# The next expert's routing and gather issued ahead of an expert's weight slices, in a mixture-of-experts layer kernel

## Chip, cores, metric

The kernel runs on one core of one Trainium2 chip. The metric is the device time of one execution in microseconds (us); the kernel before takes 2491.59 us (median of 3 runs, 2488.86 to 2494.27).

## What is computed

One layer of a diffusion backbone: a mixer over 2048 latent and 256 context tokens, then an expert-choice mixture of experts (MoE), then a final RMSNorm. The change lies in the MoE alone. Each of 16 experts takes the 256 tokens with its largest affinity, and its rows are added back, scaled by the gate:

```python
cap = EC_CAPACITY * N // N_EXPERTS            # 2 * 2048 // 16 = 256
aff = jax.nn.softmax((h @ w_router + b_router).astype(jnp.float32), axis=-1)
gate, idx = lax.top_k(jnp.swapaxes(aff, 1, 2), cap)
xe = jax.vmap(lambda hb, ib: hb[ib])(h, idx)
hid = jax.nn.silu(jnp.einsum("becd,edf->becf", xe, w_gate)) * jnp.einsum("becd,edf->becf", xe, w_up)
ye = jnp.einsum("becf,efd->becd", hid, w_down) * gate[..., None].astype(h.dtype)
return jax.vmap(lambda ib, yb: jnp.zeros((N, D), yb.dtype).at[ib.reshape(-1)].add(yb.reshape(-1, D)))(idx, ye)
```

## The kernel before

The first 1240 us are the mixer, then a threshold search for the 256 largest affinities of every expert. The MoE follows, expert by expert, all in fp32 precision made of three fp32r products: every operand is split into a rounded high part and the low rest (`mm3`, L193 to L196, three matmuls per product).

What one expert `e` does:

- **Routing**, `route(e)` (L1339): 16 one-hot pieces `oh` on VectorE (L1343), 32 small TensorE matmuls that gather token numbers and gates into the PSUM tile `c` (L1348), then on VectorE `idx` (the 256 token numbers, L1352), `rs` and `gate` (L1354 to L1357). The tiles `idx` and `gate` have two buffers each, `oh` has one.
- **Gather**, the rest of `expert_in(e)`: two indirect DMAs from POOL's queue read 128 rows each of `f_rows` into `xg` (L1373, one buffer).
- **Transposes**: 16 TensorE transposes of `xg` into the PSUM tile `xt` (L1381, two buffers of 4 transposes each), copied out as `xS[0]` by ScalarE (L1383) and `xS[1]` by VectorE (L1384). `xS` has one buffer, so half of the copies wait until the running expert's last gate/up matmul.
- **Gate and up**: `for i in range(2)`: a 512-column slice of each weight, then 4 groups of 48 matmuls into the PSUM tile `gu` (three buffers). ScalarE applies SiLU (`sgl`, L1401), VectorE multiplies (L1402), the result is split into `hS` (L1404, L1405).
- **Down**: two column slices times two halves of the tokens, 24 matmuls each into `dn`, drained by VectorE as `ye` (L1421).
- **Scatter-add**: two indirect DMAs from POOL's queue add `ye` into `h_rows` at the rows that `idx` names (L1458). The second waits until the first has landed.

A weight slice comes in two 1 MB halves: `raw` (two buffers, SP's queue, L177), rounded to `wh` on ScalarE (L183), the rest `wl` on VectorE (L184). `wh` and `wl` have three buffers (pools `wr` and `wx`).

The next expert's input is made inside the running one: `expert` calls `mid()`, which is `expert_in(e + 1)`, between the two passes of the gate/up loop (L1406):

```python
                if mid is not None and i == 0:
                    nx = mid()
```

The order in which each engine's instructions finally stand is set by the tile framework's scheduler, which replays the recorded program in a model of the engines' times. The order on an engine is fixed after that: an instruction that waits holds up all behind it on its engine.

In experts 13 and 14 the final RMSNorm of finished token tiles (`final_tile`, L1482) runs beside the weights; experts 13 to 15 read their rows of `h_rows` (`hr`, L1413) instead of adding in the DMA.

Of the kernel before, what the change touches and what calls it, by code (L numbers as in the profile page):

```python
# [39 lines left out]
def layer_kernel(ctx, tc, x, c, cx, c_ctx, w_mod, b_mod, norm1_g, norm2_g, w_in, conv_w, a_log, dt_bias,  # L40
# [1165 lines left out]

    early.close()
    moe(tc, ctx, locals())


def moe(tc, ctx, env):
# [6 lines left out]
    with ExitStack() as pd:  # L1218
# [120 lines left out]
        def route(e):  # L1339
            oh = ohp.tile([P, 2, 8, 256], BF, name="oh", bufs=1)  # L1340
            for s in range(2):
                for g in range(8):
                    nc.vector.tensor_scalar(oh[:, s, g, :], siob, SL[:, s, e, g:g + 1], None, op0=OP.is_equal)  # L1343
            rp = ps_c.tile([P, 2, 256], F32, name="c")
            for hf in range(2):
                for i in range(16):
                    s, g = divmod(i, 8)
                    nc.tensor.matmul(rp[:, hf, 0:5], oh[:, s, g, hf * P:(hf + 1) * P], vals[:, s, e, g, :],  # L1348
                                     start=(i == 0), stop=(i == 15))
            idx = rt.tile([P, 2], I32, name="idx", bufs=2)  # L1350
            with nc.allow_low_precision(reason="token numbers are whole"):
                nc.vector.tensor_reduce(idx, rp[:, :, 0:2], axis=AX.X, op=OP.add)  # L1352
            rs = rt.tile([P, 2, 5], F32, name="rs", bufs=2)
            nc.vector.tensor_copy(rs, rp[:, :, 0:5])  # L1354
            gate = rt.tile([P, 2], F32, name="gate", bufs=2)
            nc.vector.tensor_tensor(gate, rs[:, :, 2], rs[:, :, 3], op=OP.add)
            nc.vector.tensor_tensor(gate, gate, rs[:, :, 4], op=OP.add)  # L1357
            return idx, gate
# [3 lines left out]
        def next_w(src):  # L1362
            if pre:
                return pre.pop(0)
            pool = wx if nchunk[0] % 3 == 2 else wr
            nchunk[0] += 1
            return load_w(raw_p, pool, src)

        def expert_in(e):
            idx, gate = route(e)  # L1370
            xg = wk.tile([P, 2, D], F32, name="xg", bufs=1)
            for hf in range(2):
                last[1] = nc.gpsimd.indirect_dma_start(out=xg[:, hf, :], out_offset=None, in_=f_rows,  # L1373
                                                       in_offset=bass.IndirectOffsetOnAxis(ap=idx[:, hf:hf + 1], axis=0))
            xS = [wk.tile([P, KT, 256], F32R, name=f"xS{s}", bufs=1) for s in range(2)]
            for kk in range(4):
                ps = ps_t.tile([P, 2, 256], F32, name="xt")
                for k2 in range(2):
                    for hf in range(2):
                        k = 2 * kk + k2  # L1380
                        nc.tensor.transpose(ps[:, k2, hf * P:(hf + 1) * P], xg[:, hf, k * P:(k + 1) * P], ident)  # L1381
                ks = slice(2 * kk, 2 * kk + 2)
                nc.scalar.activation(xS[0][:, ks, :], ps, AF.Copy)  # L1383
                last[0] = nc.vector.tensor_tensor(xS[1][:, ks, :], ps, xS[0][:, ks, :].bitcast(F32), op=OP.subtract)  # L1384
            return idx, gate, xS

        def expert(e, st, mid=None):
            idx, gate, xS = st
            nx = None
            hS = [wk.tile([P, KT, 256], F32R, name=f"hS{s}", bufs=1) for s in range(2)]  # L1390
            for i in range(2):
                gw = next_w(w_gate[0, e, :, i * 512:(i + 1) * 512])
                uw = next_w(w_up[0, e, :, i * 512:(i + 1) * 512])
                for f in range(4):
                    fs = slice(f * P, (f + 1) * P)
                    pg = ps_a.tile([P, 2, 256], F32, name="gu")
                    for j, w in enumerate((gw, uw)):
                        for k in range(KT):
                            mm3(pg[:, j, :], w[0][:, k, fs], w[1][:, k, fs], xS[0][:, k, :], xS[1][:, k, :], k, KT)
                    sg_ = wk.tile([P, 256], F32, name="sgl", bufs=2)  # L1400
                    nc.scalar.activation(sg_, pg[:, 0, :], AF.Silu)  # L1401
                    nc.vector.tensor_tensor(sg_, sg_, pg[:, 1, :], op=OP.mult)  # L1402
                    ff = 4 * i + f
                    nc.scalar.activation(hS[0][:, ff, :], sg_, AF.Copy)  # L1404
                    nc.vector.tensor_tensor(hS[1][:, ff, :], sg_, hS[0][:, ff, :].bitcast(F32), op=OP.subtract)  # L1405
                if mid is not None and i == 0:  # L1406
                    nx = mid()
            ye = wk.tile([P, 2, D], F32, name="ye", bufs=1)
            if e >= NE - NLAST:
                hr = wk.tile([P, 2, D], F32, name="hr", bufs=1)  # L1410
# [71 lines left out]
        def final_tile(t):  # L1482
            ht = wk.tile([P, D], F32, name="ht", bufs=2)
            nc.sync.dma_start(ht, h_rows[t * P:(t + 1) * P, :])
            final_norm(ht, ht)
            nc.sync.dma_start(out[t * P:(t + 1) * P, :], ht)

        last = [None, None]
        st = expert_in(0)
        with tc.issue_after(last[1].ins):  # L1490
            pre.append(load_w(raw_p, wx, w_gate[0, 0, :, 512:1024], cast=C2))
        for e in range(NE):
            nx = mid = None
            if e + 1 < NE:
                if e in MIDE:
                    mid = lambda: expert_in(e + 1)
                else:
                    nx = expert_in(e + 1)
            for t in FTS.get(e, ()):
                final_tile(t)  # L1500
            st = expert(e, st, mid) or nx
# [98 lines left out]
```

## Time and profile before

| | us |
|---|---|
| median of 3 runs | 2491.59 (2488.86 to 2494.27) |
| the profiled execution | 2491.46 |
| its span | 2489.7 |
| TensorE busy in it | 2360.5 (95%), 16841 matmuls |
| VectorE, ScalarE, POOL busy | 1580.0, 1120.1, 516.9 |
| granted TensorE clock, mean | 0.973 |

The span is the time from the first to the last instruction in the trace. The profiled execution's own time is 1.76 us more than its span. Busy times are shares of the whole; what a stage is bound by is read from that stage. In the rows further down, a bracket at a row's end gives the idle time of that engine just before the row and what ended it.

### The profile page before, as it was taken

Reading aid. Unit: us, or ns where it says so; the run is one execution under the profiler, and the core shown is the slowest. Engines: PE = TensorE matmul, PEld = TensorE weight load, DVE = VectorE, ACT = ScalarE, POOL = GpSimd, SP = SyncE. Lnnn points to the kernel's source line nnn. Section 1 sums busy time; section 2 is a strip of 40 time slices with the busy share of each in tenths; the row PEclk is TensorE's granted clock in tenths of the full one; section 3 lists DMA queues with packets and bytes.
Section 4 is the critical chain, followed back from the end, with each engine's and each line's share of the span. In section 5 each row is a group of like instructions: output and inputs, shape, how many; then the busy total and the mean of one; then the engine's idle time right before and its main releaser. Section 6 shows DMA issues by size and latency. Waiting matters only on the chain.

```text
span 2489.7 us, 43138 instructions
## 1 busy us (share of the span) xinstructions
PE 2360.5 (95%) x16841; PEld 2160.1 (87%) x16841; DVE 1580.0 (63%) x3335; ACT 1120.1 (45%) x2008; POOL 516.9 (21%) x451
## 2 busy tenths in 40 slices
PE   7999999998988989999949999999999999999998
PEld 5999999887777888888838899999999999998897
DVE  7688755557879546566774556555565565556675
ACT  4554555567633444333332444444444444444453
POOL 2321222211112553232250101101111011111211
PEclk9999999999999999999978999999999999999999
DMA  8676655399856998655463666666676666668894
GB/s 262 200 232 199 216 164 171 124 269 323 266 127 192 253 276 235 199 180 182 166 201 111 203 187 215 199 208 207 203 220 196 210 217 199 209 205 266 300 300 166
DMA packets 487994, 526.59 MB, mean 212 GB/s; under 512 B 103887, under 2 KB 409880, under 8 KB 485742
## 3 DMA queue, kind: packets, MB, share of 16 engines
q1 hardware_dynamic: 470238, 463.27, 59.0%
q0 software_dynamic: 17120, 59.77, 8.3%
q8 instruction: 133, 2.18, 0.4%
q10 hardware_dynamic: 432, 0.79, 0.1%
q14 instruction: 71, 0.58, 0.1%
HBM read 400.45 MB, written 123.31 MB: 210 GB/s over the span
## 4 chain that ended last, share of the span: by engine, by line
PE 56%; DMA 14%; DVE 7%; ACT 4%; issue 3%; SPq 1%; POOL 1%; POOLq 0%; DVEq 0%; ACTq 0%
PE gu L196 6%; PE gu L195 6%; PE gu L194 6%; DMA xg<-f_rows,idx 4%; PE dn L195 4%; PE dn L194 4%; PE dn L196 4%; PE mx L194 2%; PE mx L195 2%; PE mx L196 2%; ACT wh L183 2%; PE pj L194 1%; PE pj L195 1%; PE pj L196 1%; DVE wl L184 1%
## 5 line engine op out<-in xcount | busy, mean ns | idle before, releaser
L184 DVE TENSOR_TENSOR wl<-raw,wh 128x2048 fp32r<-128x2048 f32 (+1 forms) x214 | 450.3, 2116 | 297.5 <-ACT wh L183 297.3
L194 PE MATMUL gu<-xS,wh 128*128 128x256 f32 x2048 | 582.3, 285 | 5.9 <-ACT wh L183 4.7
L196 PE MATMUL gu<-xS,wl 128*128 128x256 f32 x2048 | 580.8, 286 | 4.7 <-DVE wl L184 4.7
L195 PE MATMUL gu<-xS,wh 128*128 128x256 f32 x2048 | 582.1, 285 | 0.0
L183 ACT ACTIVATE wh<-raw 128x2048 fp32r<-128x2048 f32 (+1 forms) x218 | 381.6, 1771 | 361.3 <-DMA raw<-in_w_gate_dram 145.6
L194 PEld LDWEIGHTS gu<-xS,wh 128*128 128x128 f32 x2048 | 395.7, 193 | 8.0 <-ACT wh L183 5.3
L196 PEld LDWEIGHTS gu<-xS,wl 128*128 128x128 f32 x2048 | 394.5, 193 | 6.4 <-DVE wl L184 5.4
L195 PEld LDWEIGHTS gu<-xS,wh 128*128 128x128 f32 x2048 | 396.0, 193 | 1.1
L194 PE MATMUL pj<-aS,wh 128*128 128x258 f32 x832 | 239.2, 291 | 3.5 <-DVE y L460 3.1
L195 PE MATMUL pj<-aS,wh 128*128 128x258 f32 x832 | 239.9, 290 | 0.2 <-DVE aS L358 0.2
L196 PE MATMUL pj<-aS,wl 128*128 128x258 f32 x832 | 239.3, 289 | 0.9 <-DVE wl L184 0.9
L1458 POOL DMA_INDIRECT h_rows<-ye,idx x26 | 66.8, 2568 | 660.7 <-DVE ye L1421 567.8
L194 PE MATMUL dn<-wh,hS 128*128 128x512 f32 (+1 forms) x520 | 202.7, 390 | 0.0
L195 PE MATMUL dn<-wl,hS 128*128 128x512 f32 (+1 forms) x520 | 201.2, 387 | 0.4 <-DVE wl L184 0.4
L196 PE MATMUL dn<-wh,hS 128*128 128x512 f32 (+1 forms) x520 | 200.3, 386 | 0.0
L194 PEld LDWEIGHTS pj<-aS,wh 128*128 128x128 f32 x832 | 158.2, 192 | 5.0 <-issue 2.8
L195 PEld LDWEIGHTS pj<-aS,wh 128*128 128x128 f32 x832 | 160.1, 193 | 0.6 <-DVE aS L358 0.4
L196 PEld LDWEIGHTS pj<-aS,wl 128*128 128x128 f32 x832 | 159.3, 192 | 1.3 <-DVE wl L184 1.1
L194 PE MATMUL uv<-wh,ast 128*128 128x512 f32 x384 | 154.1, 401 | 0.0
L196 PE MATMUL uv<-wh,ast 128*128 128x512 f32 x384 | 151.2, 394 | 0.0
L195 PE MATMUL uv<-wl,ast 128*128 128x512 f32 x384 | 150.9, 393 | 0.0
L1404 ACT ACTIVATE hS<-sgl 128x256 fp32r<-128x256 f32 x128 | 53.1, 414 | 176.6 <-DVE sgl L1402 176.4
(480 smaller groups left out, 4547.3 us busy)
## 6 DMA issues: line engine op xcount, KB each, us to landing
raw<-in_w_gate_dram SPq DMA_DIRECT2D x64, 1024.0 KB
raw<-in_w_up_dram SPq DMA_DIRECT2D x64, 1024.0 KB
raw<-in_w_down_dram SPq DMA_DIRECT2D x64, 1024.0 KB
kv<-kv SPq DMA_DIRECT2D x140, 256.0 KB
raw<-in_w_mod_dram SPq DMA_DIRECT2D x18, 1024.0 KB
a_sp<-aS SPq DMA_DIRECT2D x32, 512.0 KB
ast<-a_sp POOLq DMA_DIRECT2D x16, 1024.0 KB, 7.8
raw<-in_w_in_dram SPq DMA_DIRECT2D x12, 1024.0 KB
```

What stands on the lines that cost most here:

```text
L183: nc.scalar.activation(wh[:, ks, s:s + 256], raw[:, ks], AF.Copy)
L184: (lo_eng or nc.vector).tensor_tensor(wl[:, ks, s:s + 256], raw[:, ks], wh[:, ks, s:s + 256].bitcast(F32), op=OP.subtract)
L194: pace(nc.tensor.matmul(ps, ah, bh, start=(k == 0), stop=False), after)
L195: nc.tensor.matmul(ps, ah, bl, start=False, stop=False)
L196: return nc.tensor.matmul(ps, al, bh, start=False, stop=(k == nk - 1))
L1404: nc.scalar.activation(hS[0][:, ff, :], sg_, AF.Copy)
L1458: nc.gpsimd.indirect_dma_start(out=h_rows, out_offset=bass.IndirectOffsetOnAxis(ap=idx[:, hf:hf + 1], axis=0), in_=ye[:, hf, :], in_offset ...
```

## The change

`expert_in(e)` is cut in two. The first part (routing and the gather) keeps the name and returns `idx`, `gate`, `xg`. The second, `turn`, holds the transposes and their copies. `expert` calls the first part ahead of its first weight slice, and `turn` where `mid()` was called.

```diff
@@ expert_in
             for hf in range(2):
                 last[1] = nc.gpsimd.indirect_dma_start(out=xg[:, hf, :], out_offset=None, in_=f_rows,
                                                        in_offset=bass.IndirectOffsetOnAxis(ap=idx[:, hf:hf + 1], axis=0))
+            return idx, gate, xg
+
+        def turn(idx, gate, xg):
             xS = [wk.tile([P, KT, 256], F32R, name=f"xS{s}", bufs=1) for s in range(2)]
...
@@ expert
             hS = [wk.tile([P, KT, 256], F32R, name=f"hS{s}", bufs=1) for s in range(2)]
+            g = mid() if mid is not None else None
             for i in range(2):
...
                 if mid is not None and i == 0:
-                    nx = mid()
+                    nx = turn(*g)
@@ the loop over experts
-        st = expert_in(0)
+        st = turn(*expert_in(0))
...
-                    nx = expert_in(e + 1)
+                    nx = turn(*expert_in(e + 1))
```

Lines behind the new `return` stand 3 or 4 higher in the changed kernel (`ye` is L1425 there, `sgl` L1406, `hS` L1409, the transposes L1384).

Experts 0 and 1 keep their order, since the scheduler had already put the routing of experts 0, 1 and 2 ahead of expert 0's weights. In experts 2 to 12 the same piece repeats, so it is shown once.

VectorE, from the fourth `ye` of expert 3 into the first gate/up groups of expert 4, before (the semaphores DMASW count transfers of POOL's queue, DMAHW those of SP's queue; `idx` is that of expert 5):

```order
L1421 SCALAR_TENSOR_TENSOR ye<-dn,gate,gt2r 128x512 [waits PE_49]
L184 TENSOR_TENSOR wl<-raw,wh 128x8x256 [waits DMAHW4_49,Activation_49]
L184 TENSOR_TENSOR wl<-raw,wh 128x8x256 [waits DMAHW5_49,Activation_49]
L1402 TENSOR_TENSOR sgl<-sgl,gu 128x256 [waits Activation_49]
L1405 TENSOR_TENSOR hS_16801<-sgl,hS_16800 128x256 [waits Activation_49]
L1402 TENSOR_TENSOR sgl<-sgl,gu 128x256 [waits Activation_49]
L1405 TENSOR_TENSOR hS_16801<-sgl,hS_16800 128x256 [waits Activation_49]
L1402 TENSOR_TENSOR sgl<-sgl,gu 128x256 [waits Activation_49]
L1405 TENSOR_TENSOR hS_16801<-sgl,hS_16800 128x256 [waits Activation_49]
L184 TENSOR_TENSOR wl<-raw,wh 128x8x256 [waits DMAHW6_49,PE_49,Activation_49]
L1352 TENSOR_REDUCE idx<-c 128x2 [waits DMASW2_49,DMASW1_49,DMASW3_49,DMASW0_49,PE_49]
L1354 COPY rs<-c 128x10
```

The same place in the changed kernel:

```order
L1425 SCALAR_TENSOR_TENSOR ye<-dn,gate,gt2r 128x512 [waits PE_49]
L1343 TENSOR_SCALAR oh<-siob,SL 128x256 [waits PE_49]
L1343 TENSOR_SCALAR oh<-siob,SL 128x256 x15
L184 TENSOR_TENSOR wl<-raw,wh 128x8x256 [waits DMAHW4_49,Activation_49]
L1352 TENSOR_REDUCE idx<-c 128x2 [waits DMASW2_49,DMASW3_49,DMASW1_49,DMASW0_49]
L1354 COPY rs<-c 128x10
L184 TENSOR_TENSOR wl<-raw,wh 128x8x256 [waits DMAHW5_49,Activation_49]
L1356 TENSOR_TENSOR gate<-rs 128x2 [waits DVE_49]
L1406 TENSOR_TENSOR sgl<-sgl,gu 128x256 [waits Activation_49]
L1357 TENSOR_TENSOR gate<-gate,rs 128x2 [waits DVE_49]
L1409 TENSOR_TENSOR hS_16801<-sgl,hS_16800 128x256 [waits Activation_49]
```

`idx` moved from behind three drained gate/up groups and three weight halves to behind one weight half, with a `wl` and all drains of the gate/up groups now behind it. It waits for the same four transfers of POOL's queue in both.

TensorE, where the last run of routing matmuls of an expert begins (`gu` is gate/up, `dn` down), before, in the middle of the first gate/up pass:

```order
L194 MATMUL gu<-xS_17098,wh 128x256
L195 MATMUL gu<-xS_17099,wh 128x256
L196 MATMUL gu<-xS_17098,wl 128x256
L1348 LDWEIGHTS oh
L1348 MATMUL c<-vals,oh 128x5
```

and in the changed kernel, behind the last down matmul of the expert before:

```order
L194 MATMUL dn<-wh,hS_16109 128x512
L195 MATMUL dn<-wl,hS_16109 128x512
L196 MATMUL dn<-wh,hS_16110 128x512
L1348 LDWEIGHTS oh
L1348 MATMUL c<-vals,oh 128x5
```

Before, 9 of an expert's 32 routing matmuls stand between two down groups and 23 behind some 190 gate/up matmuls; now 18 and 8 stand between down groups and 6 behind the last.

TensorE at the first transposes of an expert's input, before:

```order
L194 MATMUL gu<-xS_16407,wh 128x256
L195 MATMUL gu<-xS_16408,wh 128x256
L1381 MATMUL xt<-ident,xg 128x128 x2
L196 MATMUL gu<-xS_16407,wl 128x256
L194 MATMUL gu<-xS_16407,wh 128x256
```

and in the changed kernel:

```order
L195 MATMUL gu<-xS_16408,wh 128x256
L196 MATMUL gu<-xS_16407,wl 128x256
L1384 MATMUL xt<-ident,xg 128x128 x8
L194 MATMUL gu<-xS_16407,wh 128x256
L195 MATMUL gu<-xS_16408,wh 128x256
```

Before, two transposes stand behind 272 of the running expert's 384 gate/up matmuls and six more 11 matmuls later; now all eight of the first half stand behind exactly 192 of them. On POOL the order of scatter-adds and gathers is the same in both: two scatter-adds of one expert, then two gathers. On SP only some halves and token tiles of experts 13 to 15 change places.

## Rows read from the trace of the kernel before

**Rows 1.** Busy time by stretch: expert 1, experts 2 to 12, start of the tail.
```profile
core 0: us, PE busy (x) PEld busy (x) DVE busy (x) ACT busy (x) POOL busy (x), PEclk, DMA share, GB/s
1382.79:1457.98 75.19, 71.83 (x498) 67.37 (x497) 38.57 (x41) 30.31 (x32) 6.74 (x4) 0.98 0.63 196
1457.98:2240.75 782.77, 779.14 (x5809) 733.58 (x5807) 462.08 (x616) 334.07 (x352) 98.16 (x44) 1.00 0.67 207
2240.75:2312.00 71.25, 67.91 (x509) 64.19 (x508) 43.80 (x61) 32.36 (x43) 12.33 (x11) 0.98 0.83 272
```
**Rows 2.** TensorE's waits, 1457.98 to 2240.75 us: total, times, longest.
```profile
PE xt L1381 <- DMA xg<-f_rows,idx: 3.4, 7, 1.0
```
**Rows 3.** Timeline of VectorE: first a run of one-hots, then expert 1.
```profile
1324.24 3.21 DVE L1343 TENSOR_SCALAR oh<-siob,SL 128x256 bf16<-128x256 bf16 x16
...
1398.75 0.75 DVE L1421 SCALAR_TENSOR_TENSOR ye<-dn,gate,gt2r 128x512 f32<-128x512 f32 x1 [1.26 <-PE dn L196]
1401.18 2.29 DVE L184 TENSOR_TENSOR wl<-raw,wh 128x2048 fp32r<-128x2048 f32 x1 [1.68 <-ACT wh L183]
1411.82 0.16 DVE L1352 TENSOR_REDUCE idx<-c 128x2 int32<-128x4 f32 x1 [8.35 <-DMA h_rows<-ye,idx]
...
1414.45 0.41 DVE L1402 TENSOR_TENSOR sgl<-sgl,gu 128x256 f32<-128x256 f32 x1
```
**Rows 4.** Timeline of POOL, expert 1.
```profile
1394.90 1.62 POOL L1458 DMA_INDIRECT h_rows<-ye,idx  x1 [63.30 <-DVE ye L1421]
1403.42 1.58 POOL L1458 DMA_INDIRECT h_rows<-ye,idx  x1 [6.90 <-DMA h_rows<-ye,idx]
1412.77 2.58 POOL L1373 DMA_INDIRECT xg<-f_rows,idx  x1 [7.77 <-issue]
```
**Rows 5.** Timeline of TensorE, expert 1: its waits and the stretch behind them.
```profile
1414.92 0.39 PE L194 MATMUL gu<-xS,wh 128*128 128x256 f32 x1 [1.23 <-DVE sgl L1402]
...
1422.21 0.30 PE L1381 MATMUL xt<-ident,xg 128*128 128x128 f32 x1 [1.27 <-DMA xg<-f_rows,idx]
1423.38 0.98 PE L1381 MATMUL xt<-ident,xg 128*128 128x128 f32 x7 [0.86 <-DMA xg<-f_rows,idx]
1424.11 0.36 PE L194 MATMUL gu<-xS,wh 128*128 128x256 f32 x1
...
1427.69 0.32 PE L196 MATMUL gu<-xS,wl 128*128 128x256 f32 x1
```
**Rows 6.** Busy time by stretch, expert 1: right behind the waits, and later.
```profile
1424.20:1427.50 3.30, 3.30 (x19) 3.30 (x18) 0.98 (x3) 0.45 (x2) 0.00 (x0) 0.52 1.07 359
1428.00:1448.00 20.00, 20.00 (x170) 20.00 (x168) 7.17 (x9) 7.55 (x10) 0.00 (x0) 1.00 0.41 134
```
**Rows 7.** Timeline of POOL: a scatter-add pair of the long form, one of the short.
```profile
1613.38 3.42 POOL L1458 DMA_INDIRECT h_rows<-ye,idx  x1 [41.54 <-DVE ye L1421]
1624.69 2.33 POOL L1458 DMA_INDIRECT h_rows<-ye,idx  x1 [7.88 <-DMA h_rows<-ye,idx]
1639.60 1.07 POOL L1373 DMA_INDIRECT xg<-f_rows,idx  x1 [12.59 <-DVE rs L1354]
...
1684.30 1.62 POOL L1458 DMA_INDIRECT h_rows<-ye,idx  x1 [40.88 <-DVE ye L1421]
1691.84 2.52 POOL L1458 DMA_INDIRECT h_rows<-ye,idx  x1 [5.92 <-DMA h_rows<-ye,idx]
```
**Rows 8.** Timeline of VectorE: the fourth `ye` beside each of these pairs.
```profile
1616.55 0.75 DVE L1421 SCALAR_TENSOR_TENSOR ye<-dn,gate,gt2r 128x512 f32<-128x512 f32 x1 [1.23 <-PE dn L196]
...
1687.67 0.75 DVE L1421 SCALAR_TENSOR_TENSOR ye<-dn,gate,gt2r 128x512 f32<-128x512 f32 x1 [0.19 <-PE dn L196]
```
**Rows 9.** DMA issues, the scatter-add at 1624.69 us: median us to landing.
```profile
h_rows<-ye,idx POOLq DMA_INDIRECT x1, 9.8
```
**Rows 10.** TensorE's waits from 2240.75 us to the end.
```profile
PE gu L194 <- ACT wh L183: 4.7, 3, 3.2
PE gu L196 <- DVE wl L184: 4.7, 4, 1.5
```

## The prediction

> **What bounds the kernel now.** I first read busy time by stretch, cut at the same TensorE instruction of each expert. In the eleven experts 2 to 12 TensorE is busy 779.14 of 782.77 us, 70.8 of 71.2 us per expert, at a granted clock of 1.00 [rows 1]. VectorE is busy 42 us of such an expert. TensorE's waits there are all of one kind, transposes that wait for the gathered rows, 3.4 us in seven waits [rows 2]. So the wait that the change aims at is worth 3.4 us in this stretch, and what else it costs TensorE counts in full.
>
> Expert 1 takes 75.19 us, though it has no routing matmuls [rows 1]; its routing was already done ahead, and its `idx` already stands early on VectorE, behind a single weight half. Its timelines are therefore the changed order in small. `idx` could not be written at 1403.5, when VectorE came to it: it waited 8.35 us for the second scatter-add of expert 0 to land [rows 3]. The reason is the buffer: `idx` has two, so the numbers for expert e+1 go where those of expert e-1 are, which the scatter-adds of e-1 still read. Behind `idx` stood the drains of the gate/up groups. TensorE filled its three `gu` buffers, waited 1.23 us, reached the transposes, and waited 1.27 and 0.86 us more, since the gather could only leave at 1412.77, behind `idx` [rows 4, 5]: 3.36 us idle. Behind that the granted clock was 0.52, the lower of its two levels, and 17 intervals of gate/up matmuls took 3.58 us, 0.21 each, where 0.118 is normal (170 in 20 us) [rows 5, 6]: 1.6 us more.
>
> **The change part by part.** The matmuls, transposes, drains and transfers are the same in number. Four things move.
>
> 1. The gather. Before, it left at 1639.60 in an expert whose fourth `ye` began at 1616.55, 23.0 us behind [rows 7, 8]. I call that start D; it follows the last down matmul at once. The gather cannot leave before `idx`, and `idx` not before the scatter-adds have landed (time R). Expert 1: R is 1411.82, D is 1398.75, R is D+13.1 [rows 3].
>
> 2. The transposes move further than the gather does. In the new order 6 routing matmuls (some 0.2 us) and 144 gate/up matmuls stand ahead of the first one that needs a drained buffer: at 0.118 us that is D+17.2. The transposes stand behind 192: D+22.8. Before, 272 stood ahead of them.
>
> 3. `idx` in front of the drains. In expert 1 TensorE goes on 3.1 us behind R (1414.92) and has all gathered rows 11.56 us behind R (1423.38) [rows 3, 5]. So idle time per expert is R+11.56, less D+22.8, less 0.5 of useful transposing and pipeline between: R minus D minus 11.7.
>
> How large is R-D in experts 2 to 12? Their scatter-adds leave at the same point of the expert before and after the change, so the old rows tell. There are two forms. Long, in 8 of these 11: the first leaves at D-3.2, POOL needs 3.42 us for it, the second leaves 11.3 later at D+8.1 [rows 7, 8]. It lands after 9.8 us there [rows 9], after 8.4 us in expert 1, where VectorE stood still beside it [rows 3, 4]. In the new order VectorE stands still then, so I take 8.4: R is D+16.5, idle 4.8 us (6.2 with 9.8). Short, in 3 of 11: the first at D-3.4, the second 7.5 later at D+4.2 [rows 7, 8]; VectorE is then writing one-hots and a weight half, so I take 9.8: R is D+14.0, idle 2.3 us (0.9 with 8.4). The clock: a long one idles more than expert 1 did, so it pays 1.6 us; for a short one, between that and the waits of up to 1.0 us that cost no clock [rows 1, 2], half, 0.8. The ends are 0 and 3.2.
>
> Sum: 8 x (4.8 + 1.6) + 3 x (2.3 + 0.8) = 60.5 us, less the 3.4 us of old waits: +57. Expert 1's own idle and clock in all eleven would be 11 x 5.0 - 3.4 = +51, so the two agree.
>
> 4. What else moves. Sixteen one-hots (3.2 us [rows 3]) now stand ahead of a weight half right behind D. That half is needed only for the second gate/up pass, past D+22, so they cost nothing; were they late, it would be 3.2 us per expert. The weight stream stands while VectorE waits, from about D+6.5 to R, since `raw` is freed by `wl`. In expert 1 it stood 8.35 us and caught up: TensorE's waits in that expert are the three above. I take nothing, and price it below. In expert 13 the same `idx` waits once more; there weights already made TensorE wait (4.7 + 4.7 us from 2240.75 to the end [rows 10]), and a few weight halves and token tiles change places on SP. I take +2, between -4 (all gather waits of the tail gone and some weights earlier) and +8 (as for a long one in expert 13, and a little more). Experts 0 and 1 do not change.
>
> 2491.46 for the profiled execution, +57, +2: **2550 us**. The median of the runs is 0.13 us above the profiled execution, which changes nothing.
>
> **The rivals.** *The short form everywhere.* Whether the first scatter-add is long shows in VectorE's order: where a `wl` had begun before POOL's instruction, POOL took 3.42 us, else 1.62. With VectorE shifted, all eleven might be short: 11 x (2.3 + 0.8) - 3.4 + 2 = +33, 2524; with the quickest landing and no clock loss 11 x 0.9 - 3.4 = +6.5, 2498. Against it: the weight halves beside D hang on the second gate/up pass, in which nothing is held up. The Trainium skill (SBUF — State Buffer, Who interferes with whom) infers that VectorE's `tensor_tensor` does not hold up POOL's descriptor writing; by that rule the short form would hold everywhere. The two durations speak against it here.
>
> *The wait is hidden: not slower.* If the scatter-adds landed before VectorE comes to `idx` at about D+6.5 (fourth `ye` 0.75, one-hots 3.2, `wl` 2.3), nothing would stand still, the gather would leave 16 us earlier than now, and all old gather waits would go: 2491.5 - 4 = 2487. It decides at two landings of under 5 us each; the rows show 8.5 and 8.4 [rows 3, 4] and 11.3 and 9.8 [rows 7, 9]. The Trainium skill (DMA: Bandwidth & Descriptors, Anatomy of one DMA) fits 2.0 us plus bytes over 436 GB/s for a DMA of POOL's queue; my estimate from it is 3.2 us for 128 rows of 4 KB, and so this rival's time. The measured landings are over twice that, so it gets little.
>
> *The weight stream does not catch up.* `wl` behind `idx` comes 10 us later, the next `raw` with it, and TensorE waits for weights in each expert, as it does in the tail. The tail's 9.4 us lie in about three experts, 3 us each: 11 x 3 on top, 2583. For it: 10 us of stopped stream against 71.2 us for twelve halves; against it: expert 1.
>
> *The change does little.* The scheduler could have left the order as it was; the order rows show that `idx` and the transposes moved in eleven experts and that both wait for the same things as before, so this has no weight of its own.
>
> **How the numbers follow.** Forecast (long forms mostly) 0.66, 2515 to 2580; all short 0.18, 2498 to 2524; hidden 0.05, about 2487; weights late 0.11, 2570 to 2600. The range leaves out the hidden case, the lowest third of the short one and the upper half of the weights' case: 2505 to 2588. A measurement of this kernel can tell 0.2%, 5 us. Slower by more than that: all but the hidden case and a little of the short one, 0.93; within it 0.05; faster 0.02, since even all gather waits are only 4 us.
>
> **What would show it.** In the changed profile VectorE's waits list `idx` behind the scatter-add some 13 times, 7 to 10 us each, about 115 us in all, and TensorE's list the drain `sgl` and the gathered rows, about 48 us together; experts 2 to 12 take 74 to 77 us each, with a granted clock of 0.97 to 0.99. The gathers leave about 1 us behind each `idx`. I am wrong if those experts stay under 72 us, if `idx` waits but TensorE does not, or if TensorE's new waits are for `wh` and `wl`.

## The result, and the profile after

| | before | changed |
|---|---|---|
| median of 4 runs each, us | 2490.23 (2484.49 to 2494.27) | 2516.78 (2512.46 to 2521.0) |
| profiled execution, us | 2491.46 | 2519.66 |
| its span | 2489.7 | 2517.8 |
| experts 2 to 12 | 782.77 | 813.10 |
| from there to the end | 248.95 | 245.8 |

The change makes the kernel slower: ratio 1.0098, 95% interval 1.0079 to 1.0117. (Ratios are given here as they are on record with the runs; they differ from the quotient of the two medians, 1.0107 here, by up to 0.15%.) By the spans it costs 28.1 us: 30.3 in experts 2 to 12, 0.9 ahead of them, and 3.1 given back in the tail. The forecast had 59 us, over twice that.

Busy time by stretch (columns as in [rows 1]): experts 2 to 12, the start of the tail, then experts 4 and 8 alone and 3.3 us behind the transposes of each.

```profile
1458.90:2272.00 813.10, 789.12 (x5810) 733.96 (x5809) 461.19 (x617) 334.80 (x352) 89.78 (x44) 1.00 0.65 200
2272.00:2343.25 71.25, 67.87 (x514) 63.66 (x513) 45.11 (x64) 32.79 (x40) 12.21 (x11) 1.00 0.82 270
1605.18:1679.21 74.03, 71.53 (x530) 66.46 (x528) 42.22 (x57) 30.43 (x32) 8.37 (x4) 1.00 0.65 199
1900.24:1977.12 76.88, 72.98 (x529) 67.94 (x528) 42.08 (x57) 30.43 (x32) 8.49 (x4) 0.98 0.63 192
1647.20:1650.50 3.30, 3.30 (x30) 3.30 (x29) 2.08 (x3) 0.42 (x1) 0.00 (x0) 1.00 0.93 304
1943.60:1946.90 3.30, 3.30 (x19) 3.30 (x18) 0.84 (x3) 0.54 (x2) 0.00 (x0) 0.55 1.08 366
```

Against [rows 1] TensorE idles 23.98 us in the eleven experts (813.10 less 789.12) where it idled 3.63, and is busy 789.12 us where it was busy 779.14. So the 30.3 us are 20.35 of additional idle time and 9.98 of the same matmuls taking longer. The last two rows show a part of the second: behind the waits of expert 8 the granted clock was 0.55, the lower level, with 19 matmuls in 3.3 us; behind those of expert 4 it was 1.00, with 30.

What TensorE waited for in experts 2 to 12 (total, times, longest):

```profile
PE xt L1384 <- DMA xg<-f_rows,idx: 14.1, 15, 2.2
PE gu L194 <- DVE sgl L1406: 9.3, 11, 1.7
```

The first row answers to [rows 2], 3.4 us in seven waits; the second is new. What VectorE waited for at `idx`, from 1300 us to the end:

```profile
DVE idx L1352 <- DMA h_rows<-ye,idx: 73.0, 8, 10.2
DVE idx L1352 <- issue: 41.6, 5, 9.2
```

That is 114.6 us in 13 waits. "issue" means that the profile shows no releaser for five of them; they stand in the same place and are of much the same length. In the first of them `idx` starts at 1709.29 us, and the second scatter-add, which POOL begins at 1699.10, lands 10.1 us later, so there too `idx` follows the landing at once.

Expert 4 shows the chain. VectorE's timeline, from the fourth `ye` of expert 3 on:

```profile
1619.94 0.75 DVE L1425 SCALAR_TENSOR_TENSOR ye<-dn,gate,gt2r 128x512 f32<-128x512 f32 x1 [0.21 <-PE dn L196]
1620.61 3.22 DVE L1343 TENSOR_SCALAR oh<-siob,SL 128x256 bf16<-128x256 bf16 x16
1624.07 2.29 DVE L184 TENSOR_TENSOR wl<-raw,wh 128x2048 fp32r<-128x2048 f32 x1 [0.24 <-ACT wh L183]
1636.12 0.16 DVE L1352 TENSOR_REDUCE idx<-c 128x2 int32<-128x4 f32 x1 [9.77 <-DMA h_rows<-ye,idx]
```

POOL's timeline of the same expert:

```profile
1617.79 3.44 POOL L1462 DMA_INDIRECT h_rows<-ye,idx  x1 [51.23 <-DVE ye L1425]
1628.94 1.59 POOL L1462 DMA_INDIRECT h_rows<-ye,idx  x1 [7.71 <-DMA h_rows<-ye,idx]
1637.07 2.37 POOL L1373 DMA_INDIRECT xg<-f_rows,idx  x1 [6.54 <-issue]
1639.74 0.97 POOL L1373 DMA_INDIRECT xg<-f_rows,idx  x1 [0.30 <-issue]
```

TensorE's waits in it:

```profile
1639.02 0.39 PE L194 MATMUL gu<-xS,wh 128*128 128x256 f32 x1 [1.59 <-DVE sgl L1406]
1645.08 0.30 PE L1384 MATMUL xt<-ident,xg 128*128 128x128 f32 x1
1646.25 0.98 PE L1384 MATMUL xt<-ident,xg 128*128 128x128 f32 x7 [0.86 <-DMA xg<-f_rows,idx]
```

D (the start of the fourth `ye`) is 1619.94. The second scatter-add leaves 9.0 us later, and `idx` follows its landing at 1636.12, which is R, D+16.2. VectorE stands still for 9.77 us until then, the drains behind `idx` start 2.4 us later, and TensorE, out of `gu` buffers, goes on 2.9 behind R. The gather leaves 0.95 behind R and its last rows are there 10.13 behind R (1646.25).

### The profile page after: what moved, and what is told of

The parts are those of the page before. It is cut to its first block, busy times and chain, and to the rows that moved or that the text cites. A ratio compares the mean times of both kernels' runs of the same rounds, so it can differ in the third digit from the quotient of the medians.

```text
span 2517.8 us, 43148 instructions
## 1 busy us (share of the span) xinstructions
PE 2371.0 (94%) x16841; PEld 2159.3 (86%) x16841; DVE 1581.7 (63%) x3335; ACT 1121.7 (45%) x2008; POOL 510.9 (20%) x451
## 5 line engine op out<-in xcount | busy, mean ns | idle before, releaser
L194 PE MATMUL gu<-xS,wh 128*128 128x256 f32 x2048 | 583.8, 286 | 14.8 <-DVE sgl L1406 11.0
```

The source lines that it names most:

```text
L194: pace(nc.tensor.matmul(ps, ah, bh, start=(k == 0), stop=False), after)
```

## Experiments

The theory: `idx` has two buffers, so it waits until the scatter-adds that still read the old numbers have landed; VectorE, TensorE and the gather stand behind it, and everything else about the change is harmless. The first rival: the transposes have come too far forward, whatever `idx` does. The second: a cost of the new order itself, on TensorE or in the weight stream. The kernel before was run again beside each group: 2495.26 us (e1 to e4), 2497.05 (e5 to e8), 2495.22 (e9, e10). The ratios compare with these runs.

**e1: a third buffer for `idx` in the changed kernel.**

```diff
-            idx = rt.tile([P, 2], I32, name="idx", bufs=2)
+            idx = rt.tile([P, 2], I32, name="idx", bufs=3)
```

> The changed kernel with three buffers of idx instead of two, so that the numbers of expert e+1 no longer overwrite those that the scatter-adds of expert e-1 still read. Theory (the wait of idx for the scatter-adds, through its two buffers, is what costs): VectorE's waits no longer list idx behind the scatter-add, TensorE's waits for the drain sgl go, experts 2 to 12 fall from 73.9 us to 71 us, and the time to 2482 to 2492. The gathers still stand behind the second scatter-add on POOL, so a remainder of gather waits of up to 1 us per expert is allowed. Rival (the early gather itself, beside scatter-adds and weight loads, or the one-hots ahead of the weight half, slow the expert): it stays at 2510 to 2520.

Measured: 2471.84 us (2467.76 to 2477.09), ratio 0.9914, interval 0.9894 to 0.9934: 45 us under the changed kernel, and faster than the kernel before. The two waits of expert 4 above are gone in experts 2 to 12; TensorE is never idle in experts 2 to 12 (busy time by stretch, those experts):

```profile
1450.66:2222.00 771.34, 771.34 (x5800) 717.10 (x5799) 461.69 (x617) 335.45 (x352) 85.68 (x44) 1.00 0.67 210
```

VectorE around one `idx`:

```profile
1535.39 0.75 DVE L1425 SCALAR_TENSOR_TENSOR ye<-dn,gate,gt2r 128x512 f32<-128x512 f32 x1 [0.51 <-PE dn L196]
1536.06 0.15 DVE L1352 TENSOR_REDUCE idx<-c 128x2 int32<-128x4 f32 x1
```

and POOL:

```profile
1532.50 1.58 POOL L1462 DMA_INDIRECT h_rows<-ye,idx  x1 [58.88 <-DVE ye L1425]
1536.48 1.07 POOL L1373 DMA_INDIRECT xg<-f_rows,idx  x1 [2.40 <-DVE rs L1354]
1537.86 1.02 POOL L1373 DMA_INDIRECT xg<-f_rows,idx  x1 [0.30 <-issue]
1540.45 3.08 POOL L1462 DMA_INDIRECT h_rows<-ye,idx  x1 [1.57 <-DMA h_rows<-ye,idx]
```

`idx` is written 0.67 us behind D, and the gather leaves between the two scatter-adds instead of behind both. The scheduler did more with the buffer than drop a wait: it moved the routing one step further ahead. So the worth of the buffer has two parts, the wait that is gone and that new order. The result is 10 us better than the low end of what I expected, which needs the next runs.

**e2: the third buffer in the kernel before**, with nothing else changed.

> The kernel before with three buffers of idx. Theory: only expert 1 had the wait there, so expert 1 falls from 75.2 us (75.8 with routing matmuls) to about 71 us and the time by 4 to 5 us, to about 2486; the old gather waits of experts 2 to 12 (3.4 us) stay. Rival (expert 1 was slow for another reason, as the start of the stage): no change, 2490.

Measured: 2484.02 us (2481.29 to 2492.89), ratio 0.9970, 0.9957 to 0.9983. As expected, there is little to gain: in the old order the wait of `idx` for a scatter-add stands in expert 1 alone, and there it is gone. The gain is 7 us by the ratio, above the 4 to 5 expected; e6 below shows that the third buffer's shift of the tiles gives about as much by itself.

**e3: the scatter writes instead of adding**, in the changed kernel, so the scatter lands sooner and `idx` still waits for it. The sum over the experts is left out, so the kernel no longer computes the layer; the order of instructions on every engine is that of the changed kernel.

```diff
-                                                 in_=ye[:, hf, :], in_offset=None, compute_op=OP.add)
+                                                 in_=ye[:, hf, :], in_offset=None)
```

> The changed kernel with scatters that write instead of add (the sum over experts is left out), in the same order of instructions on every engine. Theory (the landing of the two scatter-adds sets when idx can be written): if a plain scatter lands sooner, at 4 to 6 us each instead of 11 and 6.5, idx waits 0 to 3 us instead of 9, TensorE waits for nothing new, and the time is 2485 to 2497. If it lands as late as with the add, the time stays near 2515 and idx waits as long. Rival (the wait of idx is not what TensorE loses its time to): idx waits less and the time stays.

Measured: 2483.95 us (2475.75 to 2489.13), ratio 0.9953, 0.9938 to 0.9968. VectorE's and TensorE's waits from 1300 us to the end:

```profile
DVE idx L1352 <- DMA h_rows<-ye,idx: 63.4, 12, 6.7
DVE idx L1352 <- issue: 3.0, 1, 3.0
PE xt L1384 <- DMA xg<-f_rows,idx: 4.9, 5, 1.9
```

VectorE still waits 66 us at `idx`, in the longer ones over twice the 0 to 3 us each that I expected, and yet TensorE waits only 4.9 us for gathered rows, 0.6 of it in experts 2 to 12. So VectorE's wait is not what costs; what costs is the part of it that outlasts TensorE's stock of work. In expert 4 of this kernel R is D+12.8, 3.4 us sooner than with the add, and TensorE is not idle there at all. The order on VectorE and TensorE is that of the changed kernel, and the kernel is no slower than the one before, which speaks against the second rival. What the plain scatter saves by itself is not told apart here.

**e4: the transposes behind 218 gate/up matmuls instead of 192**, one group into the second pass as the scheduler lays it out.

```diff
-                if mid is not None and i == 0:
-                    nx = turn(*g)
+                    if mid is not None and i == 1 and f == 0:
+                        nx = turn(*g)
```

> The changed kernel with the transposes one group later: behind 218 gate/up matmuls of an expert instead of 192, 3.1 us later on TensorE. Theory: the gathered rows land about 26 us behind the last down matmul, TensorE then comes at about 27 us, so the waits for the gather (14 us in experts 2 to 12) and the two drops of the clock go, the waits for the drain (9 us) and that of idx stay: 2497 to 2505. Rival (TensorE loses its time to the drains alone, and the gather's waits only take over what would be lost anyway): 2512 to 2518.

Measured: 2497.55 us (2490.1 to 2504.91), ratio 1.0006, 0.9991 to 1.0021. Waits from 1300 us to the end:

```profile
DVE idx L1352 <- DMA h_rows<-ye,idx: 70.4, 8, 9.8
DVE idx L1352 <- issue: 42.8, 5, 9.3
PE gu L194 <- DVE sgl L1406: 7.7, 10, 1.6
PE xt L1384 <- DMA xg<-f_rows,idx: 2.9, 2, 1.9
```

`idx` waits as long as in the changed kernel (113.2 us), the transposes no longer wait in experts 2 to 12, and 19 us come back by the medians, 23 by the ratios. So the first rival has a part: 26 matmuls, 3 us of work, decide whether a late gather is seen.

**e5 to e10: is it the buffer, or where it pushes the tiles?** By the program's layout the third `idx` buffer takes 32 bytes per partition, and `oh`, `xg`, `xS`, `hS`, `sgl` and `ye` stand 32 bytes further on. In e1 the matmuls themselves had changed: gate/up ran quicker, down slower. So e5 and e6 add 32 unused bytes to the changed kernel and to the one before, with the same instructions in the same order on every engine:

```diff
-        SL = rt.tile([P, 2, NE, 8], F32, name="SL", bufs=1)
+        SL = rt.tile([P, 2 * NE * 8 + 8], F32, name="SL", bufs=1)[:, 0:256].rearrange("p (s e g) -> p s e g", s=2, e=NE)
```

e5, the changed kernel with it:

> The changed kernel with two idx buffers and the same instructions in the same order on every engine; only SL is 32 bytes longer per partition, so that xS, hS, xg and ye start 32 bytes further on, where the third idx buffer put them. In the trace of e1_idx3 a gate/up matmul takes 116.5 ns and a down matmul 235.1, against 120.4 and 229.7 in the changed kernel. Theory A (the place of the tiles sets these times, not the third buffer and not the order): gate/up 116 to 117 ns, down 233 to 236; the first pass is hidden behind the wait for the scatter-add in any case, so per expert only the second pass gains, 192 x 3.9 ns = 0.75 us, against 96 x 5.4 = 0.5 us lost: 2510 to 2518, idx waits as before, TensorE's waits longer by some 8 us. Theory B (order or buffer): 120 ns and 2515 to 2520.

Measured: 2513.98 us (2509.2 to 2518.73), ratio 1.0077, 1.0056 to 1.0099. Costliest groups of TensorE from 1440 to 2240 us (matmuls, busy us, mean ns of one), the changed kernel:

```profile
L195 PE MATMUL gu<-xS,wh 128*128 128x256 f32 x1373 | 389.4, 284 | 0.0
L195 PE MATMUL dn<-wl,hS 128*128 128x512 f32 x352 | 137.3, 390 | 0.0
```

and e5:

```profile
L195 PE MATMUL gu<-xS,wh 128*128 128x256 f32 x1395 | 389.9, 280 | 0.0
L195 PE MATMUL dn<-wl,hS 128*128 128x512 f32 x352 | 139.2, 395 | 0.0
```

Matmuls overlap, so a mean includes the pipeline; from start to start e5's take about 117 ns (gate/up) and 235 (down) against 120 and 230. Neither the order nor the buffer does this, since both are those of the changed kernel. The `idx` wait stays (111.8 us), and with it the loss; TensorE's waits for gathered rows and for the drain together grow by 0.8 us, where I had put down some 8.

e6, the kernel before with it:

> The kernel before with the same 32 bytes and nothing else. Theory A: gate/up 117.5 ns instead of 120.5, down 233 instead of 227.6, so per expert 384 x 3.0 ns less and 96 x 5.5 ns more, 0.6 us less; times 16 experts about 10 us: 2480 to 2486, as with the third idx buffer, which then had no worth of its own there but expert 1's wait. Theory B (the third buffer or the order): the time of before, 2490 to 2495, with 120.5 ns.

Measured: 2492.0 us (2481.24 to 2495.78), ratio 0.9974, 0.9958 to 0.9990. The matmuls changed as expected (about 117 and 234 ns), the time by half of what I had put down: it is above the 2480 to 2486 expected. TensorE's waits for gathered rows, from 1300 us to the end:

```profile
PE xt L1381 <- DMA xg<-f_rows,idx: 17.4, 17, 2.1
```

In the kernel before, the same view has 8.9 us in 12 waits: a TensorE that is sooner at the transposes waits longer there for a gather that leaves no sooner, which would account for the half that is missing.

e7, three `idx` buffers and the 32 bytes (64 further on in all), and e9, the same with 96 bytes (128 further on):

> The changed kernel with three idx buffers and the 32 bytes more, so that xS and hS stand at a multiple of 64 bytes again, as in the kernel before and the changed one; the order is that of e1_idx3. This takes the worth of the buffer apart from that of the place. Theory A: gate/up 119 to 120.5 ns, down 228 to 230, 0.8 us more per expert than e1_idx3: 2482 to 2487, so the change with its idx wait taken away is worth 5 to 10 us against before, about the gather waits. Theory B (the quicker matmuls came from the new TensorE order): as e1_idx3, 2470 to 2476.

> e1_idx3 with SL 96 bytes longer, the same instructions in the same order. With the 32 bytes of the third idx buffer xS and hS are 128 bytes further on than in the changed kernel; in e7_idx3_even they were 64 bytes further on, and gate/up still took 117.3 ns and down 235.3. Theory A (the place modulo 128 bytes sets the matmul times): gate/up 119 to 120.5 ns, down 228 to 230, an expert 70.7 to 70.9 us instead of 70.1 to 70.5, the whole 2476 to 2486, and no wait for a scatter-add: that is the worth of the buffer alone. Theory B (any kernel with the third idx buffer has the quick gate/up and the slow down matmuls): 117 and 235 ns, 2470 to 2476.

Measured: e7 2473.18 us (2472.12 to 2481.67), ratio 0.9913, 0.9890 to 0.9935, with about 118 and 235 ns; e9 2475.7 us (2471.24 to 2482.11), ratio 0.9921, 0.9899 to 0.9943, with about 119 and 235 ns. I had expected 120 and 229 again, by the remainder of the place modulo 64 and then 128 bytes; both rules are refuted.

e8 and e10 are e1 with `xS1` 32 and 96 bytes longer, which moves `hS` but not `xS`:

> As e1_idx3, with xS1 32 bytes longer, so that xS keeps its place (32 bytes past a multiple of 64) and hS goes back to a multiple of 64, where down matmuls took 228 to 230 ns. If hS's place sets the down matmul: 228 to 230 ns instead of 235.1 with gate/up still at 116.5, 96 x 6 ns = 0.6 us per expert, 9 us in 16: 2461 to 2465, the fastest of all. If the down matmul's time comes from something else: 235 ns and 2470 to 2476.

> e1_idx3 with xS1 96 bytes longer, so that xS stands where gate/up took 116.5 ns and hS at the same place modulo 128 bytes as in the kernel before, where down took 227.6 to 229.7 ns; same instructions, same order. If the places of xS and hS act each by itself: 117 and 229 ns, 96 x 6 ns = 0.6 us less per expert than e1_idx3, 2461 to 2466. If not: 2470 to 2476.

Measured: e8 2470.85 us (2464.8 to 2475.63), ratio 0.9896, 0.9872 to 0.9920; e10 2471.34 us (2462.22 to 2475.33), ratio 0.9903, 0.9879 to 0.9928. Down stays at about 235 ns in both, so the place of `hS` by itself does not set it. That the place acts is shown by e5 and e6; which tile and which property of its address is open, and every shift tried gave 117 to 119 ns for gate/up and 233 to 236 for down.

What these settle, with e1 and e2, is the account of the buffer. With the tiles 32 bytes further on in all four:

| ratio to before | `idx` x 2 | `idx` x 3 |
|---|---|---|
| old order | 0.9974 (e6) | 0.9970 (e2) |
| new order | 1.0077 (e5) | 0.9914 (e1) |

In the old order the third buffer is worth nothing that the ratios can tell (6 us by the medians, where the runs of either kernel spread over 11 us and more). In the new one it is worth 1.6%, some 41 us. And with the wait away the new order is worth 0.56%, 14 us (12 by the medians): where e1 has no idle time in experts 2 to 12, e2 has 9.3 us of it, and 2.2 more of busy time, in part since the granted clock fell once, to 0.50 from 2067.5 to 2070.8 us (busy time by stretch):

```profile
1449.17:2232.07 782.90, 773.59 (x5800) 722.22 (x5799) 462.88 (x617) 334.23 (x352) 94.47 (x44) 1.00 0.67 207
```

So the change does what it says once `idx` has somewhere to go, and then none of its loss is left. The loss takes two things together, an `idx` that is held and transposes that come behind 192 matmuls: e1 takes away the one, e4 the other, and either is enough.

## Why the prediction was right in direction and wrong in size

The step that failed is the idle time of part 3, "R minus D minus 11.7", which gave 45.3 us where 23.4 were measured; the clock term that was put on top of every wait went with it, 15.2 us where some 3 were.

- **The mechanism: right.** `idx` waits behind the scatter-adds 13 times, 114.6 us (forecast: some 13, about 115). TensorE's waits are the two that were named, 23.4 us together in experts 2 to 12 and 3.8 in expert 1, where some 48 were forecast; those experts take 73.9 us each on average, just under the 74 to 77 forecast. The gather leaves 0.95 us behind `idx` (forecast: about 1).
- **R-D: near on average.** The eleven lie between D+14.5 and D+16.3, 15.3 on average; the forecast had 16.5 (long) and 14.0 (short), 15.8 on average. Both forms were off, in opposite directions: 15.6 and 14.8. In three of the short ones VectorE is still at a `wl` when the last down matmul ends, so that D is up to 0.7 us behind it. In the long form the second scatter-add leaves some 1 us later than before (D+9.0 in expert 4, D+8.1 in [rows 7, 8]) and lands in 6.1 to 7.2 us instead of 8.4; the short form lands in 9.5 to 10.4 (9.8). There were 7 long ones and 4 short ones, so the rival with short forms everywhere did not come. The Trainium skill (SBUF — State Buffer, Who interferes with whom) infers that VectorE's `tensor_tensor` does not hold up POOL's descriptor writing; the trace disagrees again: 3.44 us on POOL where a `wl` was running when the scatter-add began, about 1.6 where none was. The same section of the Trainium skill says that an instruction with two inputs in SBUF, as `wl` is, contends with reads by POOL; which of the two acts here no run shows.
- **Idle time, 8 x 4.8 + 3 x 2.3 = 45.3 us: this step failed, 23.4 measured.** For expert 4 "R minus D minus 11.7" gives 16.2 - 11.7 = 4.5 us, and the rows show 1.59 + 0.86 = 2.45. What went into the 11.7 is taken apart below.
- **The clock, 15.2 us: failed too, some 3 measured.** TensorE's busy time grew by 9.98 us, and not all of it is the clock. Only experts 8 and 9 fell to the lower level behind their waits, with 72.98 and 72.91 us of busy TensorE instead of 71.5, some 3 us in both. The forecast took the fall from expert 1, where it followed 3.36 us of waits. In the changed kernel expert 1 waits 1.69 + 1.17 + 0.94 = 3.80 us, and there the granted clock stays at 1.00 (busy time behind its transposes):

```profile
1426.00:1429.30 3.30, 3.30 (x29) 3.30 (x30) 2.36 (x2) 1.17 (x2) 0.00 (x0) 1.00 0.92 305
```

  Starting again after a wait costs about 0.26 us more than the wait itself (1.87 us between two matmuls of expert 4, less the wait of 1.59, less 0.12, and 0.10 more at the next): by this estimate from one wait, 26 waits now and seven before make some 5 us that the forecast had no term for. About 2 us I have not located.
- **The tail, +2 with an end of -4: -3.1 measured.** The waits there sum to 9.9 us, 10.4 before, and the first expert takes 71.25 us in both. The other 2.6 us are busy time: from the end of expert 12 on TensorE is busy 226.95 us where it was 229.62, at a granted clock of 0.99 instead of 0.97. Whether the change brings that about no run shows.
- **The weight stream: right.** No wait for `wh` or `wl` in experts 2 to 12, though VectorE stands still 9 us in each.
- **The hidden rival: its mechanism is what e1 builds.** The forecast gave the worth of a free gather as the old gather waits, 4 us, and 2487. At equal places it is 12 to 14 us (e1 against e2), as the gather waits there are larger.

The 11.7 came from expert 1, the one place where the changed order could be seen ahead of the change. There the last gathered rows came 11.56 us behind R [rows 3, 5]. In expert 4 they came 10.13 behind it, and over the eleven 10.54 on average (10.1 to 10.6 in eight, 11.4 in three). The DMA issues of the two gathers (median us to landing), in expert 1 of the kernel before:

```profile
xg<-f_rows,idx POOLq DMA_INDIRECT x2, 8.5
```

and in expert 4 of the changed kernel:

```profile
xg<-f_rows,idx POOLq DMA_INDIRECT x2, 7.2
```

That is 1.0 us per expert, 11 of the 21.9 us by which the term is too large. R-D, 15.3 instead of 15.8, is some 6 more. The rest, some 5, is the stock of work: between D and the last transposes TensorE worked 23.86 us in expert 4 (26.31 less the 2.45 of waiting) and 23.7 on average, where the forecast had 22.8 + 0.5, since a gate/up matmul took 0.120 us there and not 0.118, and the restart came on top. The idle time is what 26 us, until the gathered rows are there, leave over 24 us of work: an error of 4% in either is half of it. The direction was no luck, since the waits that were named are the ones that came. That the size was not further off is luck in part: the restarts, which the forecast left out, made up for some of what it had too large.

## What to carry to other kernels

Before issuing a step earlier, ask which buffer it writes and who still reads the last contents; an index tile that an indirect DMA reads is held until that DMA has landed, and one more buffer (32 bytes here) turned a loss of 0.8% into a gain of 0.9% with the tiles at equal places (e5 and e1). When a new wait is weighed against a stock of work nearly as long, give the difference a range and read the terms from a stage like the one to come, not from one instance. When an edit changes the size of a tile, look at the mean time of unchanged instructions before crediting the edit: run the old order with the same padding.

## What the runs showed of the hardware that was not expected

- 32 unused bytes ahead of the operand tiles, with the same instructions in the same order, made gate/up matmuls some 2.5% quicker (120 to 117 ns) and down matmuls 2% slower (230 to 235), in the changed kernel (e5) and in much the same way in the one before (e6).
- The clock fell behind 1.72 + 1.32 + 0.86 = 3.90 us of waits (expert 8) and 0.55 + 1.35 + 0.86 = 2.76 (expert 9), and not behind 1.69 + 1.17 + 0.94 = 3.80 (expert 1), 0.47 + 2.15 = 2.62 (expert 7) or 1.59 + 0.86 = 2.45 (expert 4). With expert 9 below expert 1, the sum of the waits does not by itself tell whether the level falls.
- A scatter that writes instead of adding lands 5.2 us after POOL begins it in expert 4 of e3, where the adding one took 7.2, and POOL spends 2.79 and 0.98 us on the pair instead of 3.44 and 1.59.
